# Chunk states from three rounded products, and one sum per half block read from PSUM, in a hybrid SSD and attention trunk

## The chip, the cores and the metric

The kernel runs on one core of one Trainium2 chip. The metric is the device time of one execution in microseconds, taken as the median of several runs. Engines are named as the profile does: PE is the matrix engine (PEld its weight loads), DVE the vector engine, ACT the scalar engine, POOL the GpSimd engine, SP the engine that issues most DMAs. On-chip memory is SBUF; products land in PSUM, which has banks of 128 x 512 float32.

## The reference

The model is a two-layer decoder trunk on 1040 tokens (16 learned meta tokens and 1024 of the sequence), width 1024. Layer 0 is a state-space mixer (Mamba-2 style, "SSD") and a gated feed-forward block with a width-3 causal convolution; layer 1 is stick-breaking attention and another such block. All is float32. Two parts matter here.

In the mixer there are 32 heads of 64 in four groups of eight; each group shares its B and C (128 states). Cut into chunks of tokens, a chunk computes

```
cb[l,s]       = sum_n C[l,n] B[s,n]
y_diag[l,h,p] = sum_s cb[l,s] * exp(a_cs[l,h]-a_cs[s,h]) * xdt[s,h,p]     (s <= l)
S[n,h,p]      = sum_l B[l,n] * exp(a_end[h]-a_cs[l,h]) * xdt[l,h,p]       (chunk state)
state         = state * exp(a_end) + S
y_off[l,h,p]  = sum_n C[l,n] * exp(a_cs[l,h]) * state_before[n,h,p]
```

In the feed-forward block, `h = conv3(u @ w_up)` is cut into two halves `g` and `val` of 2816 columns, and `silu(g) * val` goes through `w_down`.

## The kernel before

**Rounded products.** PE multiplies operands of type float32r in one pass. To keep float32 precision, the kernel writes an operand as high plus low part (high is a rounded copy made by ACT, low is the difference, made by DVE or POOL), and `mm3` (L206) adds three products: high x high, high x low, low x high. Most of the work of the kernel goes through `mm3`. Small products of the mixer are plain float32 products instead: `cb`, the chunk state `S` (L801) and the outputs `y` (L812, L814).

**The mixer.** After the first blocks, `mixer` (L825) walks over 4 groups of 9 chunks (116 tokens, the last 112). Between the parts of a chunk it places units of other work from a generator `work`: one unit is one projection of a block of 128 columns on a third of the tokens, 24 products through `mm3`, followed by a convolution (L336 on ACT, L339 on DVE, a silu at L616) or, for gate blocks, a silu (L648), a product (L655), a square (L660) and a sum (L664, L666). `SHARES` (L74) says how many units a chunk takes: two in groups 0 and 3 with a few exceptions at the ends, three or four in groups 1 and 2. The first unit of a block also issues the weights of the next block: a DMA, an ACT copy (L196) and four POOL pieces (L102, tile `wl`).

A chunk has these parts. `ssd_decays` (L735) is a generator in three steps: it loads two tiles `D` and `E` by DMA; then DVE makes differences (L754) and ACT the exponential (L755); then POOL multiplies `E` with C in four pieces. `ssd_front` (L761) makes `cb` and transposes B and x on PE, copies B to SBUF on ACT (`bk`, L780), masks `cb` (L782), makes `xdt` (L784) and the decay matrix (L785) on DVE, and the inputs decayed to the chunk's end (`xde`, two pieces) on POOL. `ssd_back` (L791) makes `S` on PE, adds it to the state on DVE (L807), makes `y` on PE, adds it to x (L816) and scales the state on POOL. The loop at L873 runs front of chunk c, then the units, then back of chunk c; while the units run, the decays of chunk c+1 are stepped, one step a unit, and what is left of them is run ahead of the next front.

All of this stands in a region whose order on PE, DVE, ACT and POOL is the order in which the program issues it. Every engine takes its instructions in that order, so a waiting instruction holds what stands behind it.

**The up projection.** `up` (L1203) does the product with `w_up` as a scheme of seven products on quarter matrices in place of eight. For each of 22 blocks and each half `t` of the tokens, `block` makes the products 0 to 6 in three PSUM banks x, y, z, with sums between: `p1 = copy(x)`, `y += p1`, `u2 = copy(y)`, `p5 = copy(z)`, `z += u2` (the third sum), then product 4 is added to y, and `p5 += y` by way of a copy `u3` (L1256), and product 5 to z and product 6 to y. Copies are ACT's (L1236), sums DVE's (L1239). The two halves alternate product by product, except in block 0, where half 0 runs alone, because the operands of half 1 (`forms`, L1077) are still being made: `forms` scales the rows with the norm's factors (L1093), makes differences (`minus`, L1117) and splits them into high parts (L1099, ACT) and low parts (L1100, DVE). It is a generator too, stepped once after each product of half 0. In block 0's half 0 the convolutions are put off (`late`). Outside the mixer's and the attention's regions a planner orders the instructions of each engine ahead of time, from their dependencies and its own costs; `behind` (L200) gives it an extra order between two instructions.

Of the kernel before, what the change touches and what calls it, by code (L numbers as in the profile page):

```python
# [8 lines left out]
F32 = mybir.dt.float32  # L9
# [4 lines left out]
P = 128  # L14
# [91 lines left out]
class Trunk:  # L106
# [628 lines left out]
    def ssd_decays(self, g, ct, c, pool):  # L735
# [19 lines left out]
        nc.scalar.activation(dk, dk, AF.Exp)  # L755
        yield
        if c:
# [3 lines left out]
    def ssd_front(self, g, x, bt, ct, c, dk, pool):  # L761
# [16 lines left out]
        if c < 8:  # L778
            bk = pool.tile([P, P], F32, tag="bk", name=self.nm("bk"), bufs=2)
            nc.scalar.activation(bk[:n], pcb[:n, P : 2 * P], AF.Copy)  # L780
        cbm = pool.tile([P, CB], F32, tag="cbm", name=self.nm("cbm"), bufs=2)
# [4 lines left out]
        if c < 8:  # L786
            xde = pool.tile([P, GH, 64], F32, tag="xde", name=self.nm("xde"), bufs=2)
            pieces(nc.gpsimd, xde[:n], xdt[:n], self.cols[:n, 2, cc, h0 : h0 + GH].unsqueeze(2).to_broadcast([n, GH, 64]), ALU.mult)
        return xdt, xde, bk

    def ssd_back(self, g, x, c, dk, ce, xdt, xde, bk, states, pool):  # L791
# [7 lines left out]
        if c < 8:  # L799
            ps = self.lg("S")  # L800
            nc.tensor.matmul(ps, bk[:n], xde[:n].rearrange("p h d -> p (h d)"), start=True, stop=True)  # L801
            psv = ps.rearrange("p (h d) -> p h d", h=GH)
            if c == 0:
                new = pool.tile([P, GH, 64], F32, tag="state", name=self.nm("state"), bufs=2)
                nc.scalar.activation(new, psv, AF.Copy)
            else:
                nc.vector.tensor_tensor(new, new, psv, op=ALU.add)  # L807
# [17 lines left out]
    def mixer(self, mx):  # L825
# [12 lines left out]
        with self.tc.tile_pool(name="ssd", bufs=3) as pool:  # L838
# [27 lines left out]
            with self.tc.manual_schedule(engines={E.PE, E.DVE, E.Activation, E.Pool}):  # L866
                ahead = self.ssd_decays(0, rows[0][5], 0, pool)
                dk, ce = next(ahead)
                for g in range(GROUPS):
                    *x, bt, ct = rows[g]  # L870
                    share, given = SHARES[g], 0
                    state = None, None
                    for c in range(9):  # L873
                        if g == c == 0:
                            next(work)
                            given = 1
                        for _ in ahead:
                            pass
                        begun = False
                        ops = self.ssd_front(g, x, bt, ct, c, dk, pool)  # L880
                        now = dk, ce
                        for _ in range(sum(share[: c + 1]) - given):
                            next(work)
                            if not begun:
                                begun = True
                                nxt = (g, ct, c + 1) if c < 8 else (g + 1, rows[g + 1][5], 0) if g < 3 else None
                                ahead = self.ssd_decays(*nxt, pool) if nxt else iter([(None, None)])
                                dk, ce = next(ahead)
                            else:
                                next(ahead, None)  # L890
                            given += 1
# [185 lines left out]
    def forms(self, layer, h, r, t, tiles, pool):  # L1077
# [11 lines left out]

        def product(ks, part):  # L1090
            c = slice(new.start, s.start + N) if part == 0 else slice(s.start + N, new.stop)
            for k in ks:
                nc.vector.scalar_tensor_tensor(h[k][:, c], h[k][:, c], self.par(gain, k), r[:, c], op0=ALU.mult, op1=ALU.mult)  # L1093

# [26 lines left out]
        if t:  # L1121
            product(range(KD // 2, KD), 0)
            yield
            product(K, 1)
            yield
            t1 = minus(b12, b11)
            product(range(KD // 2, KD), 1)
            yield
            t2 = minus(b22, t1)
# [73 lines left out]
    def up(self, layer, w0, forms, rest, pool):  # L1203
# [8 lines left out]
        def block(b, t, w, late=None):  # L1212
# [35 lines left out]
            p5 = copy(z)  # L1248
            add(z, z, u2)
            yield  # L1250
# [4 lines left out]
            yield  # L1255
            u3 = copy(product(4, y, False))  # L1256
            run(lambda: (add(p5, p5, u3), made.update(v1=conv(p5, 1, 1))))
# [809 lines left out]
```

## Time and profile before

| | us |
|---|---|
| median of 3 runs | 2845.09 (2844.49 to 2850.29) |
| the profiled execution | 2848.77 |
| its span in the trace | 2847.0 |
| PE busy | 2806.7 |
| DVE busy | 2071.6 |
| ACT busy | 1582.8 |
| POOL busy | 1572.9 |
| mean granted clock of PE | 0.997 |

The span is counted from the first to the last instruction of the profiled execution. The mixer's chunk loop lies between about 115 and 615 us, the up projection of layer 0 between about 830 and 1290 us, that of layer 1 between about 2150 and 2610 us. In rows of the time line, the first two numbers are the start and the duration; in groups of instructions of one line, min/median/max are in ns; in rows of stretches, the first column after the stretch is its length, then busy time of PE, PEld, DVE, ACT and POOL with the number of instructions, then the granted clock, the DMA share and GB/s.

### The profile page before, as it was taken

What the parts mean: (1) busy time and instruction counts of PE and PEld (TensorE: products, weight loads), DVE (VectorE), ACT (ScalarE), POOL (GpSimd) and SP (SyncE); (2) the same over time, 40 slices, a digit from 0 to 9 for tenths busy, and PEclk for the clock granted to TensorE, in tenths of its full rate; (3) what the DMA queues carried; (4) which work ended last, traced back from release to release, by engine and by line L of the source; (5) the groups of instructions that cost most, each with busy time, mean ns of one, the idle gap of its engine ahead of it and who ended that gap; (6) DMA issues with size and microseconds to landing.
All of it is one profiled execution on the core that took longest, in us unless ns stands there. A gap on an engine that the chain in (4) does not pass through costs nothing. (4 is left out here: it accounts for less than half of the span.)

```text
span 2847.0 us, 56457 instructions
## 1 busy us (share of the span) xinstructions
PE 2806.7 (99%) x21251; PEld 2690.8 (95%) x21251; DVE 2071.6 (73%) x3936; ACT 1582.8 (56%) x3077; POOL 1572.9 (55%) x2144
## 2 busy tenths in 40 slices
PE   8999999999999999999999999999999999999998
PEld 7989999999999999999999999999898999999888
DVE  5676666668487676767886888888759676667786
ACT  5555554543256565655335777777646555555433
POOL 2366455553519888867763111112354888886881
PEclk9999999999999999999999999999999999999999
DMA  4333333343412222235142222322532222225331
GB/s 119 88 112 97 116 84 124 117 137 101 116 68 95 78 79 79 78 129 181 44 153 75 77 67 71 85 70 55 186 132 82 83 75 82 75 83 185 111 104 67
DMA packets 141740, 281.78 MB, mean 99 GB/s; under 512 B 16307, under 2 KB 71740, under 8 KB 141468
## 3 DMA queue, kind: packets, MB, share of 16 engines
q1 hardware_dynamic: 135844, 267.01, 29.6%
q0 software_dynamic: 2048, 6.49, 0.6%
q10 hardware_dynamic: 3576, 4.67, 0.5%
q8 instruction: 168, 2.75, 0.4%
q14 instruction: 104, 0.85, 0.1%
HBM read 207.79 MB, written 55.42 MB: 92 GB/s over the span
## 5 line engine op out<-in xcount | busy, mean ns | idle before, releaser
L102 POOL TENSOR_TENSOR wl<-w,wh 128x256 fp32r<-128x256 f32 x760 | 676.3, 921 | 345.4 <-ACT wh L196 225.8
L209 PE MATMUL pj<-uh,wh 128*128 128x348 f32 (+2 forms) x1536 | 501.1, 327 | 3.4 <-DVE xbc L339 1.4
L210 PE MATMUL pj<-ul,wh 128*128 128x348 f32 (+2 forms) x1536 | 494.8, 322 | 0.8 <-DVE ul L320 0.8
L211 PE MATMUL pj<-uh,wl 128*128 128x348 f32 (+2 forms) x1536 | 491.9, 320 | 0.0
L209 PE MATMUL p<-bh,fh 128*128 128x262 f32 (+1 forms) x1408 | 401.6, 285 | 7.1 <-DVE p L1239 3.7
L211 PE MATMUL p<-bh,fl 128*128 128x262 f32 (+1 forms) x1408 | 401.4, 285 | 0.9 <-POOL fl L102 0.9
L210 PE MATMUL p<-bl,fh 128*128 128x262 f32 (+1 forms) x1408 | 399.6, 284 | 0.1
L102 POOL TENSOR_TENSOR fl<-x,fh 128x256 fp32r<-128x256 f32 x352 | 263.6, 783 | 192.9 <-ACT fh L1176 167.0
L210 PE MATMUL p<-bl,wh 128*128 128x262 f32 (+1 forms) x1040 | 295.6, 284 | 1.1 <-DVE bl L1100 1.1
L209 PEld LDWEIGHTS pj<-uh,wh 128*128 128x128 f32 x1536 | 288.7, 188 | 7.5 <-DVE qs L1607 3.1
L209 PE MATMUL p<-bh,wh 128*128 128x262 f32 (+1 forms) x1040 | 295.4, 284 | 0.4 <-ACT ft L1236 0.4
L211 PE MATMUL p<-bh,wl 128*128 128x262 f32 (+1 forms) x1040 | 294.3, 283 | 0.0
L210 PEld LDWEIGHTS pj<-ul,wh 128*128 128x128 f32 x1536 | 289.2, 188 | 2.4 <-DVE ul L320 1.4
L339 DVE SCALAR_TENSOR_TENSOR c<-p,params,c 128x260 f32<-128x260 f32 (+1 forms) x528 | 248.4, 480 | 57.4 <-ACT c L336 50.9
L211 PEld LDWEIGHTS pj<-uh,wl 128*128 128x128 f32 x1536 | 288.7, 188 | 0.1
L209 PEld LDWEIGHTS p<-bh,fh 128*128 128x128 f32 x1408 | 268.5, 191 | 8.1 <-DVE p L1239 4.1
L211 PEld LDWEIGHTS p<-bh,fl 128*128 128x128 f32 x1408 | 267.6, 190 | 1.7 <-POOL fl L102 1.3
L210 PEld LDWEIGHTS p<-bl,fh 128*128 128x128 f32 x1408 | 268.4, 191 | 0.5 <-DVE bl L1100 0.3
L1236 ACT ACTIVATE ft<-p 128x262 f32<-128x262 f32 (+1 forms) x352 | 133.6, 382 | 180.9 <-DVE p L1239 110.9
L210 PE MATMUL acc<-gl,wh 128*128 128x260 f32 (+1 forms) x672 | 214.2, 320 | 0.0
L211 PE MATMUL acc<-gh,wl 128*128 128x260 f32 (+1 forms) x672 | 213.2, 319 | 0.0
L209 PE MATMUL acc<-gh,wh 128*128 128x260 f32 (+1 forms) x672 | 210.8, 320 | 0.1
(337 smaller groups left out, 7689.2 us busy)
## 6 DMA issues: line engine op xcount, KB each, us to landing
w<-in_w_up SPq DMA_DIRECT2D x88, 512.0 KB
w<-in_w_down SPq DMA_DIRECT2D x44, 512.0 KB
w<-in_w_in SPq DMA_DIRECT2D x40, 512.0 KB
E<-ea_d SPq DMA_DIRECT2D x32, 464.0 KB
D<-acs_d SPq DMA_DIRECT2D x32, 420.5 KB
g<-c SPq DMA_DIRECT2D x88, 130.0 KB
g<-c SPq DMA_DIRECT2D x88, 128.0 KB
b<-g SPq DMA_DIRECT2D x16, 520.0 KB
```

Source lines behind the costliest of these rows:

```text
L102: done.append(eng.tensor_tensor(out[:, c], x[:, c], y[:, c], op=op))
L209: self.behind(mm(out, wh, uh, start=first, stop=False, skip_group_check=joins), tie, "behind the sums of squares")
L210: mm(out, wh, ul, start=False, stop=False, skip_group_check=joins)
L211: self.last_mm = mm(out, wl, uh, start=False, stop=last, skip_group_check=joins)
L339: ins = nc.vector.scalar_tensor_tensor(out, ps[:, o + i : o + i + n], wcol(i), out, op0=ALU.mult, op1=ALU.add)
L1236: nc.scalar.activation(s[:, :N], ps[:, :N], AF.Copy)
```

## The change

Three parts.

1. The chunk state `S`: `bk` and `xde` are split into high and low parts (`bk` with its low part made by DVE from PSUM; `xde` high on ACT and low on DVE, in a new function `split_xde` called at the end of the front), and `S` is made by `mm3` on them. The buffers are single.
2. In the chunk loop, the last step of the decays of a chunk (POOL's `E` pieces), where it has not run between units, is issued behind the front, so behind `xde`; only the step with DVE's differences and ACT's exponential must be ahead of the front.
3. In the up projection, `p5 += u3` reads bank y itself instead of a copy of it, except in half 0 of block 0; and in `forms` for half 1, the second set of four row products and the differences behind it are issued one step later, with the four products ordered behind the third sum of block 0's half 0 on DVE.

```diff
@@ ssd_decays
-        yield
+        yield "decays"
@@ ssd_front
-            bk = pool.tile([P, P], F32, tag="bk", name=self.nm("bk"), bufs=2)
-            nc.scalar.activation(bk[:n], pcb[:n, P : 2 * P], AF.Copy)
+            bk = pool.tile([P, 2, P], F32R, tag="bk", name=self.nm("bk"), bufs=1)
+            nc.scalar.activation(bk[:n, 0], pcb[:n, P : 2 * P], AF.Copy)
+            tt(bk[:n, 1], pcb[:n, P : 2 * P], bk[:n, 0].bitcast(F32), op=ALU.subtract)
...
-            xde = pool.tile([P, GH, 64], F32, tag="xde", name=self.nm("xde"), bufs=2)
-            pieces(nc.gpsimd, xde[:n], xdt[:n], self.cols[:n, 2, cc, h0 : h0 + GH].unsqueeze(2).to_broadcast([n, GH, 64]), ALU.mult)
+            xde = [pool.tile([P, GH, 64], dt, tag=t, name=self.nm(t), bufs=1) for t, dt in (("xdh", F32R), ("xdl", F32R), ("xde", F32))]
+            pieces(nc.gpsimd, xde[2][:n], xdt[:n], self.cols[:n, 2, cc, h0 : h0 + GH].unsqueeze(2).to_broadcast([n, GH, 64]), ALU.mult)
+            self.split_xde(xde, c)
         return xdt, xde, bk
+
+    def split_xde(self, xde, c):
+
+        hi, lo, t = (t[: CH[c][1]] for t in xde)
+        self.nc.scalar.activation(hi, t, AF.Copy)
+        self.nc.vector.tensor_tensor(lo, t, hi.bitcast(F32), op=ALU.subtract)
@@ ssd_back
-            nc.tensor.matmul(ps, bk[:n], xde[:n].rearrange("p h d -> p (h d)"), start=True, stop=True)
+            hi, lo = (t[:n].rearrange("p h d -> p (h d)") for t in xde[:2])
+            self.mm3(ps, bk[:n, 0], bk[:n, 1], hi, lo, True, True)
@@ mixer
+                        if not decayed:
+                            next(ahead)
+                        begun = False
+                        ops = self.ssd_front(g, x, bt, ct, c, dk, pool)
                         for _ in ahead:
                             pass
-                        begun = False
-                        ops = self.ssd_front(g, x, bt, ct, c, dk, pool)
...
+                                decayed = nxt is None
                             else:
-                                next(ahead, None)
+                                decayed |= next(ahead, None) == "decays"
@@ forms
-        def product(ks, part):
+        def product(ks, part, tie=None):
...
+                self.behind(ins, tie, "behind the third sum")
...
             product(K, 1)
             yield
+            yield
+            product(range(KD // 2, KD), 1, self.third_sum)
             t1 = minus(b12, b11)
-            product(range(KD // 2, KD), 1)
-            yield
             t2 = minus(b22, t1)
@@ up, block
-            add(z, z, u2)
+            self.third_sum = add(z, z, u2)
...
-            u3 = copy(product(4, y, False))
+            product(4, y, False)
+            u3 = y if late is None else copy(y)
             run(lambda: (add(p5, p5, u3), made.update(v1=conv(p5, 1, 1))))
```

More of the change, by code (lines that the diff above doesn't have):

```diff
@@ L868, in mixer @@
                 dk, ce = next(ahead)
+                decayed = False
                 for g in range(GROUPS):
@@ L1088, in forms @@
         b11, b12, b21, b22 = [[b[:, c] for b in rows] for rows in (b1, b2) for c in (slice(0, N), slice(FN, N2))]
-        def product(ks, part):
+        def product(ks, part, tie=None):
             c = slice(new.start, s.start + N) if part == 0 else slice(s.start + N, new.stop)
             for k in ks:
-                nc.vector.scalar_tensor_tensor(h[k][:, c], h[k][:, c], self.par(gain, k), r[:, c], op0=ALU.mult, op1=ALU.mult)
+                ins = nc.vector.scalar_tensor_tensor(h[k][:, c], h[k][:, c], self.par(gain, k), r[:, c], op0=ALU.mult, op1=ALU.mult)
+                self.behind(ins, tie, "behind the third sum")
         last = [self.after_factors, None]
```

## The prediction

> **What bounds the kernel now.** I read the page first, then busy time by stretch, then the time lines of the engines round one chunk of the state-space part.
>
> ```profile
> span 2847.0 us, 56457 instructions
> PE 2806.7 (99%) x21251; PEld 2690.8 (95%) x21251; DVE 2071.6 (73%) x3936; ACT 1582.8 (56%) x3077; POOL 1572.9 (55%) x2144
> ```
> ```profile
> 137.00:203.00 66.00, 66.00 (x513) 60.70 (x513) 49.37 (x128) 38.00 (x52) 45.20 (x64) 1.00 0.40 115
> 2188.00:2206.00 18.00, 14.82 (x113) 14.64 (x112) 14.96 (x22) 9.77 (x20) 15.11 (x22) 0.91 0.23 81
> ```
>
> TensorE is busy for 99% of the span, so only two things can shorten it: less matmul time, or one of the few places where PE stands still. In the first stretch (chunks 2 to 7 of group 0) PE never idles, but DVE is busy 49.37 of 66 us, so its slack is 25% and no more. The second stretch, in the up projection of layer 1, is the largest stall behind the start: 3.2 us idle and the granted clock at 0.91.
>
> **The change part by part: the state product.**
>
> ```profile
> L801 PE MATMUL S<-xde,bk x64: 590/592/697, 122.6 to 596.8; 116*128 116x512 f32 x64
> ```
> ```profile
> 145.17 1.02 PE L801 MATMUL S<-xde,bk 116*128 116x512 f32 x2
> ...
> 156.44 1.02 PE L801 MATMUL S<-xde,bk 116*128 116x512 f32 x2
> 157.39 0.42 PE L812 MATMUL y<-D,xdt 116*64 116x116 f32 x4
> ```
> ```profile
> 2649.68 0.40 PE L209 MATMUL acc<-gh,wh 128*128 128x512 f32 x1
> ...
> 2650.37 0.40 PE L209 MATMUL acc<-gh,wh 128*128 128x512 f32 x1
> ```
>
> The 32 float32 products are 64 records, two passes each, and hold PE for 157.39 - 156.44 = 0.95 us. Three rounded products of the same width come 0.69 us apart as a set (2649.68 to 2650.37). I add the 0.09 us by which 0.95 exceeds two passes of 0.43 (the step to the narrow y weights): 0.79 us. So PE work falls by 0.16 x 32 = 5.1 us. This counts only where PE is what the chunk waits for.
>
> **The split in front of it.** One chunk of group 0, DVE, then ACT, then POOL; the first POOL row is chunk 0, where nothing stood ahead of the inputs:
>
> ```profile
> 150.87 0.27 DVE L782 TENSOR_TENSOR cbm<-cb,past 116x116 f32<-116x116 f32 x1
> 151.06 0.68 DVE L784 TENSOR_TENSOR xdt<-px,cols 116x512 f32<-116x512 f32 x1
> 151.66 1.27 DVE L785 TENSOR_TENSOR D<-D,cbm 116x928 f32<-116x928 f32 x1
> 153.47 1.81 DVE L339 SCALAR_TENSOR_TENSOR xbc<-pj,params,xbc 128x348 f32<-128x348 f32 x3 [0.55 <-ACT xbc L336]
> 157.31 1.80 DVE L339 SCALAR_TENSOR_TENSOR xbc<-pj,params,xbc 128x344 f32<-128x344 f32 x3 [2.02 <-ACT xbc L336]
> 159.03 1.60 DVE L754 TENSOR_SCALAR D<-D,cols 116x116 f32<-116x116 f32 x8
> ...
> 162.12 0.28 DVE L782 TENSOR_TENSOR cbm<-cb,past 116x116 f32<-116x116 f32 x1
> ```
> ```profile
> 152.80 0.64 ACT L336 ACTIVATE xbc<-pj,params 128x348 f32<-128x348 f32 x1 [2.25 <-PE pj L211]
> 153.46 1.28 ACT L616 ACT_TABLE_LOAD   x1
> 154.75 0.50 ACT L616 ACTIVATE xbc<-xbc 128x348 f32<-128x348 f32 x1
> 156.64 0.64 ACT L336 ACTIVATE xbc<-pj,params 128x344 f32<-128x344 f32 x1 [1.39 <-PE pj L211]
> ...
> 161.70 1.06 ACT L196 ACTIVATE wh<-w 128x1024 fp32r<-128x1024 f32 x1
> ```
> ```profile
> 120.52 2.00 POOL L102 TENSOR_TENSOR xde<-xdt,cols 116x256 f32<-116x256 f32 x2 [14.44 <-DVE xdt L784]
> ```
> ```profile
> 151.26 3.50 POOL L102 TENSOR_TENSOR E<-E,xbc 128x232 f32<-128x232 f32 x4
> 154.72 1.18 POOL L102 TENSOR_TENSOR xde<-xdt,cols 116x256 f32<-116x256 f32 x2
> ```
>
> Today xde ends at 155.90 and S starts at 156.44, behind four E pieces of 3.50 us. The change puts xde ahead of E, but adds three links: an ACT copy of 116x512 (0.60 us, an estimate: a little over half of the 1.06 us of the 128x1024 copy), a DVE subtraction of 116x512 (0.68 us, by xdt), and the low part of bk (0.27 us, by cbm, 0.20 us of which DVE is held). All of them are issued in the front part, so behind the waiting copy on ACT stand the weight copy, the first taps (L336), the table load and the silu of the next units; behind the waiting subtraction on DVE stand the other taps (L339), the next decays (L754), the state sum and the skip. These lead to the next chunk's xdt. That is a ring through DVE, POOL and ACT in which PE takes no part.
>
> Its length for this chunk, from cbm to cbm: bk's low part 0.20, cbm to xdt 0.19, xdt to xde 0.76 (its 0.68 and a handover), xde 2.00 because D x cbm runs beside it, handover and copy 0.65. Then ACT decides: L336, table load, silu and L336 again take 0.55 + 1.28 + 0.42 + 0.64 = 2.89, and DVE's second taps start 0.05 later (DVE itself would be free 0.5 us sooner). Then DVE alone: 159.03 - 157.31 = 1.72 for the taps and 162.12 - 159.03 = 3.09 for decays, state and skip. The sum is 11.55 us. Where a weight copy (1.06 us) stands in it, 12.6; a block has three units and a chunk two, so that is two chunks in three: 12.3 on average. PE's step today is 156.44 - 145.17 = 11.27 us. So PE, which sits 1.1 us ahead of the low part's end at first (156.67 for the second product against 150.87 + 0.20 + 0.19 + 0.76 + 2.00 + 0.65 + 0.05 + 0.68 = 155.40, with some 0.2 for handovers), loses about 1.0 us a chunk in six chunks, less that 1.1: +4.9 us. Chunk 0 waited for xde already and now waits for copy and subtraction: 1.33 less 0.16 and what the second and third products overlap, +1.0. Chunk 1 +0.5. Chunk 8 has one unit and waits for DVE already; by the same delay +2.0:
>
> ```profile
> 210.44 0.42 PE L812 MATMUL y<-D,xdt 112*64 112x112 f32 x3 [1.47 <-DVE D L785]
> ```
>
> **Group 0: 4.9 + 1.0 + 0.5 + 2.0 = +8.4 us.**
>
> Group 3 has the gate units in the same place:
>
> ```profile
> 557.69 0.46 ACT L648 ACTIVATE z<-pj 128x348 f32<-128x348 f32 x1 [1.22 <-PE pj L211]
> ```
> ```profile
> 558.57 0.80 DVE L666 TENSOR_TENSOR z<-z,z 128x344 f32<-128x344 f32 x1 [1.98 <-ACT z L660]
> 559.29 0.93 DVE L655 TENSOR_TENSOR xbc<-xbc,z 128x348 f32<-128x348 f32 x1
> 562.35 0.92 DVE L666 TENSOR_TENSOR z<-z,z 128x348 f32<-128x348 f32 x1 [2.13 <-ACT z L660]
> ...
> 566.72 0.27 DVE L782 TENSOR_TENSOR cbm<-cb,past 116x116 f32<-116x116 f32 x1
> ```
>
> Ring: 3.80 to the copy's end as above, table load 1.28, z to L666 0.88, L666 and L655 0.72 + 0.93, square and handover 0.51, then 566.72 - 562.35 = 4.37: 12.5 us, more with a weight copy, against the 11.27 of a two-unit chunk. Seven chunks would lose 9 us, but the group starts with several us of slack (its first chunks come after three units); I take **+4 us** (bounds 0 and 9). Groups 1 and 2 have three or four units a chunk, 15 to 19 us, so the ring has room: there the 16 x 0.16 = 2.6 us are gained, less about 0.9 each for a PSUM bank that a late first tap may hold: **-0.8 us**. The moved E pieces (3.5 us) end about 5.5 us after xdt, still before y needs them. The single buffers of bk and the split cost nothing: their reader, S of the chunk before, precedes cb on PE. The mixer in all: 8.4 + 4 - 0.8 = +11.6 us, bounds -7 (no ring, and the few waits for xde gone) and +20.
>
> **The sum from the bank.**
>
> ```profile
> L1239 DVE TENSOR_TENSOR p<-p,ft x176: 417/435/440, 835.1 to 2595.7; 128x262 f32<-128x262 f32 x88, 128x258 f32<-128x258 f32 x88
> L1239 DVE TENSOR_TENSOR ft<-ft,ft x88: 415/827/5627, 844.6 to 2599.9; 128x262 f32<-128x262 f32 x44, 128x258 f32<-128x258 f32 x44
> ```
> ```profile
> 2191.20 5.96 DVE L1239 TENSOR_TENSOR ft<-ft,ft 128x258 f32<-128x258 f32 x2
> ```
> ```profile
> 2202.69 0.55 PE L209 MATMUL p<-bh,fh 128*128 128x258 f32 x1 [3.18 <-ACT c L1227]
> ```
>
> In 86 of 88 half blocks the ACT copy of the fourth product goes, and the sum reads PSUM: 0.83 us becomes 0.44. Nearly all of it lies under PE, so it is worth nothing, but one of these sums took 5.6 us beside POOL's work, and its late result led to the 3.2 us stall; and at a granted clock of 0.91 over 18 us another 1.6 to 1.7 us went. A sum with a PSUM operand never passed 0.44 us. So **-5.1 us** against the profiled execution. The next reader of that bank, product 6, starts three products later, 4 us, so the later release has cover.
>
> [...]
>
> **The third sum.**
>
> ```profile
> 2153.65 3.26 DVE L1093 SCALAR_TENSOR_TENSOR h<-h,params,r 128x256 f32<-128x256 f32 x8
> 2156.82 1.44 DVE L1117 TENSOR_TENSOR ft<-h 128x258 f32<-128x258 f32 x4
> 2158.17 0.43 DVE L1239 TENSOR_TENSOR p<-p,ft 128x258 f32<-128x258 f32 x1
> ```
> ```profile
> 2158.66 0.39 PE L209 MATMUL p<-bh,fh 128*128 128x258 f32 x1 [1.84 <-DVE p L1239]
> ```
> ```profile
> 2165.92 2.51 DVE L1100 TENSOR_TENSOR bl<-h,bh 128x514 fp32r<-128x514 f32 x4
> ```
>
> The sum moves ahead of four products and four differences, 1.6 + 1.4 us, and the 1.84 us wait goes. But DVE runs without a break here, the same work ends at the same time, and PE next needs these low parts, up to 2168.4. The wait moves on, it does not go: 0, bounds -4 (both layers in full) and +1.
>
> **Sum.** 2848.77 (the profiled execution, 3.7 us over the runs' median of 2845.09) + 11.6 - 5.1 + 0 = **2855.3 us**; if the median runs had no such long sum, the mixer alone gives 2856.7 from 2845.09.
>
> **Rivals.** *The ring fits under PE* (faster): the split is done before S comes. Then -5.1, some -1.9 for xde waits, -5.1, up to -4: 2832.7. For it: DVE idles 0.55 + 2.02 us in the chunk shown. Against: those waits are for PE's projections and are spent by the 1.7 us that DVE waits for the copy. *xde runs at 1.18 us instead of 2.00* (same): the ring is 0.8 shorter, 11.5 on average, which leaves about +3 in group 0, nothing in group 3 and the -0.8, the whole 2845.9. It decides if D x cbm leaves POOL alone; 120.52 speaks against it. *The low part is blocked by the E pieces* (slower yet): with 0.5 us more in each of 14 chunks, 2862.3.
>
> Chances: forecast 0.50, blocked low part 0.13, fast xde 0.22, ring hidden 0.15. So slower by over 0.2% (5.7 us, about what this kernel's measurement can tell) 0.63, within 0.22, faster 0.15. The range 2839 to 2866 reaches into the second and third rival; that of the forecast alone is 2850 to 2862.
>
> **What would show it.** Right: PE waits before S (L801's successors) on ACT's copy and DVE's low part in groups 0 and 3, with chunk steps over 12 us there and 0.16 us shorter in groups 1 and 2; no sum on L1239 over 0.5 us in up; the third sum some 3 us earlier and a new wait for bl. Wrong: no PE wait before S, or xde at 1.2 us beside D x cbm.

## The result, and the profile after

The changed kernel takes **2871.42 us** (median of five runs, 2870.69 to 2876.17) against 2844.49 us for the kernel before on the same chip: a ratio of 1.0094, 95% interval 1.0082 to 1.0105. It is slower, as forecast, but by 27 us where 10 were forecast, and outside the range given (2839 to 2866). The profiled execution of it took 2876.17 us. The head of its page, and busy time by stretch for most of chunks 2 to 7 of group 0 (columns: stretch, length, busy time and count of PE, PE's weight loads, DVE, ACT and POOL, granted PE clock, DMA share, GB/s):

```profile
span 2874.4 us, 56436 instructions
PE 2818.0 (98%) x21283; PEld 2705.3 (94%) x21283; DVE 2079.3 (72%) x4000; ACT 1568.0 (55%) x3023; POOL 1571.3 (55%) x2144
```
```profile
148.00:218.00 70.00, 66.36 (x525) 60.38 (x523) 56.58 (x136) 40.15 (x57) 46.81 (x64) 1.00 0.41 101
```

PE, never idle in these chunks before, now stands 3.6 us of 70; DVE has gone from 75% to 81%. The time lines of DVE, ACT, POOL and PE round chunk 3 of group 0:

```profile
157.42 0.26 DVE L783 TENSOR_TENSOR cbm<-cb,past 116x116 f32<-116x116 f32 x1
157.61 0.68 DVE L785 TENSOR_TENSOR xdt<-px,cols 116x512 f32<-116x512 f32 x1
158.21 1.11 DVE L786 TENSOR_TENSOR D<-D,cbm 116x928 f32<-116x928 f32 x1
161.06 1.13 DVE L797 TENSOR_TENSOR xdl<-xde,xdh 116x512 fp32r<-116x512 f32 x1 [1.74 <-ACT xdh L796]
162.11 3.61 DVE L339 SCALAR_TENSOR_TENSOR xbc<-pj,params,xbc 128x348 f32<-128x348 f32 x6
165.64 1.60 DVE L754 TENSOR_SCALAR D<-D,cols 116x116 f32<-116x116 f32 x8
...
168.93 0.27 DVE L783 TENSOR_TENSOR cbm<-cb,past 116x116 f32<-116x116 f32 x1
...
181.41 0.26 DVE L783 TENSOR_TENSOR cbm<-cb,past 116x116 f32<-116x116 f32 x1
```
```profile
160.39 0.63 ACT L796 ACTIVATE xdh<-xde 116x512 fp32r<-116x512 f32 x1 [3.49 <-POOL xde L102]
160.93 0.62 ACT L336 ACTIVATE xbc<-pj,params 128x348 f32<-128x348 f32 x1
```
```profile
158.43 1.93 POOL L102 TENSOR_TENSOR xde<-xdt,cols 116x256 f32<-116x256 f32 x2 [0.75 <-DVE xdt L785]
160.32 3.04 POOL L102 TENSOR_TENSOR E<-E,xbc 128x232 f32<-128x232 f32 x4
```
```profile
161.08 0.51 PE L209 MATMUL S<-xdh,bk 116*128 116x512 f32 x1 [0.41 <-ACT xdh L796]
162.24 0.50 PE L210 MATMUL S<-xdl,bk 116*128 116x512 f32 x1 [0.66 <-DVE xdl L797]
```

The ring is there, link by link: xdt, xde at 1.93 us beside D x cbm, the copy xdh, the low part xdl, then six taps in a row, decays, and the next cbm 11.51 us later. The copy waits for xde, xdl for the copy, and PE for both. From chunk 1 on the steps from cbm to cbm are 12.47, 12.88 and 11.51 us in turn, 12.3 on average, as forecast. Longer than in the forecast is xdl: 1.13 us beside POOL's E pieces instead of 0.68 (a rival had foreseen it).

Where the 27 us lie can be read from the start of each S product in the two traces, which is the same place of the work. The shift of S (after less before) is 8.59 us at chunk 7 of group 0, 13.31 at chunk 0 of group 1, 21.67 at chunk 0 of group 3 and 27.90 at chunk 7 of group 3; all behind it together is 0.5 us shorter. So the mixer costs 27.9 us, not 11.6: group 0 with its chunk 8 +13.3 (forecast 8.4), groups 1 and 2 +8.4 (forecast -0.8), group 3 +6.2 (forecast 4). About 0.6 us of the first term lies ahead of the chunk loop: the kernel with the mixer alone, below, has a shift smaller by that much from the first S on.

Two things hold most of the difference. First, some of the new waits of PE are followed by a lower granted clock. PE's waits for y of chunk 8 of group 0, for the squares' sum and for a held bank in group 1, and stretches behind the first and the last:

```profile
221.27 0.56 PE L821 MATMUL y<-D,xdt 112*64 112x112 f32 x2 [3.44 <-DVE D L786]
...
285.86 0.56 PE L676 MATMUL ms<-z,ones 128*128 128x348 f32 x1 [1.06 <-DVE z L666]
...
339.26 0.58 PE L209 MATMUL pj<-uh,wh 128*128 128x348 f32 x1 [2.54 <-DVE xbc L339]
```
```profile
221.27:225.00 3.73, 3.73 (x34) 3.45 (x35) 1.92 (x5) 1.20 (x1) 0.00 (x0) 0.50 0.09 36
339.26:342.70 3.44, 3.44 (x12) 3.44 (x13) 3.37 (x7) 1.66 (x2) 3.44 (x7) 0.51 0.11 18
```

After a wait of 2.54 us PE works for 3.44 us at half the clock (0.51 in the row), which by that clock is 1.7 us more, an estimate. Between 104 and 640 us the trace of before has no stretch under full clock; the changed kernel has five (from 137.9, 219.9, 339.3, 489.5 and 574.8 us). Each is 3.41 or 3.42 us long by half-microsecond stretches of the same view, the second twice that. Half of each, taken over the time in which PE worked (the second began 1.4 us before PE did), makes 1.7 + 2.7 + 1.7 + 1.7 + 1.7 = 9.5 us, an estimate.

Not all of that stays in the total. Behind the first stretch PE waits again at S of chunks 3, 5 and 6 (0.41, 0.20 and 0.57 us for the copy), so there the ring sets its time, and the ring did not get longer by the stretch: the kernel without E products, below, has no stretch there and the same steps from cbm to cbm. That leaves at most 7.8 us, and no run tells apart how much of these stayed.

Second, a chunk of three units in groups 1 and 2 has a ring too. DVE and POOL between two chunks of group 1:

```profile
316.43 0.27 DVE L783 TENSOR_TENSOR cbm<-cb,past 116x116 f32<-116x116 f32 x1
...
324.19 3.80 DVE L754 TENSOR_SCALAR D<-D,cols 116x116 f32<-116x116 f32 x8
...
333.07 0.27 DVE L783 TENSOR_TENSOR cbm<-cb,past 116x116 f32<-116x116 f32 x1
```
```profile
324.73 2.62 POOL L102 TENSOR_TENSOR E<-E,xbc 128x232 f32<-128x232 f32 x4
```

From cbm to cbm it is 333.07 - 316.43 = 16.64 us, against 14.94 for PE's step between S of chunks 4 and 5. The eight decays L754 take 3.80 us beside POOL's weight pieces and E pieces (1.60 us in the rows of group 0 above). After two such chunks the first unit's taps are late, the bank is held, and PE waits, once each in groups 1 and 2: 2.54 and 2.52 us, some 4.2 us each time with the stretch at half clock.

In the up blocks both edits do what they say, and nothing comes of it. The group of the sums from the bank, the one long DVE instruction of layer 0 and PE behind it, and PE's waits at the third sum's place:

```profile
L1253 DVE TENSOR_TENSOR ft<-ft,p x86: 408/421/429, 886.5 to 2627.0; 128x262 f32<-128x262 f32 x43, 128x258 f32<-128x258 f32 x43
```
```profile
903.09 5.56 DVE L339 SCALAR_TENSOR_TENSOR c<-ft,params,c 128x260 f32<-128x260 f32 x1
```
```profile
909.04 0.39 PE L209 MATMUL p<-bh,wh 128*128 128x262 f32 x1 [3.30 <-DVE ft L1253]
...
872.55 0.39 PE L209 MATMUL p<-bh,fh 128*128 128x262 f32 x1 [0.92 <-ACT bh L1113]
877.36 0.39 PE L209 MATMUL p<-bh,wh 128*128 128x262 f32 x1 [0.36 <-ACT ft L1250]
878.47 0.47 PE L210 MATMUL p<-bl,wh 128*128 128x262 f32 x1 [0.71 <-DVE bl L1114]
```

The sums are at 0.42 us and none over 0.43. A 5.6 us instruction is there all the same: a tap on L339, one of those that read ft from SBUF, and PE waits 3.30 us behind it. The third sum's wait in layer 0 (1.87 us in the trace of before) has become waits for bh, ft and bl.

### The profile page after: what moved, and what is told of

Same layout as the page of the kernel before. It is cut to its first block, busy times and chain, and to the rows that moved or that the text cites. A ratio compares the mean times of both kernels' runs of the same rounds, so it can differ in the third digit from the quotient of the medians.

```text
span 2874.4 us, 56436 instructions
## 1 busy us (share of the span) xinstructions
PE 2818.0 (98%) x21283; PEld 2705.3 (94%) x21283; DVE 2079.3 (72%) x4000; ACT 1568.0 (55%) x3023; POOL 1571.3 (55%) x2144
## 4 chain that ended last, share of the span: by engine, by line
PE 77%; DVE 11%; ACT 5%; POOL 4%; issue 3%; DMA 1%; DVEq 0%; ACTq 0%; POOLq 0%
PE p L209 10%; PE p L211 10%; PE p L210 10%; PE acc L209 8%; PE acc L211 8%; PE acc L210 8%; PE pj L209 5%; PE pj L210 4%; PE pj L211 4%; PE po L1727 2%; PE lg L1670 2%; DVE D L754 2%; PE wT L1704 2%; DVE kp L1681 2%; DVE xbc L339 1%
## 5 line engine op out<-in xcount | busy, mean ns | idle before, releaser
L339 DVE SCALAR_TENSOR_TENSOR c<-p,params,c 128x260 f32<-128x260 f32 (+1 forms) x528 | 248.8, 479 | 84.5 <-ACT c L336 81.1
L209 PEld LDWEIGHTS pj<-uh,wh 128*128 128x128 f32 x1536 | 290.0, 189 | 13.3 <-ACT xbc L336 7.2
L1253 DVE TENSOR_TENSOR p<-p,ft 128x262 f32<-128x262 f32 (+1 forms) x176 | 76.4, 435 | 182.2 <-ACT ft L1250 125.1
```

Of the source, the lines that this page charges most:

```text
L209: self.behind(mm(out, wh, uh, start=first, stop=False, skip_group_check=joins), tie, "behind the sums of squares")
L339: ins = nc.vector.scalar_tensor_tensor(out, ps[:, o + i : o + i + n], wcol(i), out, op0=ALU.mult, op1=ALU.add)
L1253: add = lambda o, x, y: tt(o[:, :N], x[:, :N], y[:, :N], op=ALU.add)
```

## The experiments

My theory at the start: all of the loss is in the mixer, through the order in which the split is queued on ACT and DVE; the products save 0.16 us each; the up blocks are neutral. "Shift" below is that of S against the trace of before, in us, at four places:

| kernel | median us | ratio to before (95%) | g0 c7 | g1 c0 | g2 c7 | g3 c7 |
|---|---|---|---|---|---|---|
| changed | 2871.42 | 1.0094 (1.0082, 1.0105) | 8.59 | 13.31 | 21.84 | 27.90 |
| mixer alone | 2871.90 | 1.0088 (1.0075, 1.0101) | 7.96 | 12.70 | 21.17 | 27.17 |
| up blocks alone | 2845.53 | 0.9998 (0.9990, 1.0007) | 0.67 | 0.71 | 0.71 | 0.68 |
| products without split | 2840.16 | 0.9985 (0.9974, 0.9996) | -0.89 | -0.68 | -3.17 | -4.19 |
| order on POOL alone | 2844.95 | 0.9996 (0.9987, 1.0005) | -0.66 | 1.41 | 1.42 | 0.56 |
| late split | 2847.69 | 1.0007 (0.9998, 1.0016) | 2.62 | 4.82 | 2.32 | 4.39 |
| late split, E first | 2852.51 | 1.0026 (1.0016, 1.0037) | 6.33 | 6.31 | 3.81 | 8.72 |
| late low part alone | 2888.25 | 1.0151 (1.0136, 1.0165) | 12.59 | 13.18 | 25.35 | 41.87 |
| E first | 2893.62 | 1.0173 (1.0159, 1.0187) | 21.87 | 24.01 | 33.50 | 48.53 |
| groups 1 and 2 alone | 2841.73 | 0.9992 (0.9983, 1.0001) | -0.36 | -0.36 | -2.85 | -3.04 |
| no E products | 2856.29 | 1.0044 (1.0030, 1.0058) | 7.81 | 10.75 | 8.27 | 11.76 |
| no table loads | 2868.96 | 1.0086 (1.0072, 1.0100) | 4.77 | 9.56 | 18.18 | 24.56 |
| neither | 2852.25 | 1.0028 (1.0019, 1.0038) | 2.43 | 4.28 | 1.79 | 5.67 |

Rows two to five, six to nine and ten to thirteen each shared a chip with runs of the kernel before, whose medians there were 2845.45, 2844.82 and 2844.41 us. The longer runs of before reach 2850.7 us.

### The change taken apart

Mixer alone: the up blocks of before under the changed mixer (cut, against the changed kernel).

```diff
+            t1 = minus(b12, b11)
+            product(range(KD // 2, KD), 1)
             yield
-            product(range(KD // 2, KD), 1, self.third_sum)
-            t1 = minus(b12, b11)
             t2 = minus(b22, t1)
...
-            product(4, y, False)
-            u3 = y if late is None else copy(y)
+            u3 = copy(product(4, y, False))
```

> Only the chunk states (split, three products, decayed inputs ahead of E) are changed; the up blocks are those of before. Theory (the loss is all in the mixer: the ring through DVE, POOL and ACT in groups 0 and 3, plus waits for held banks in groups 1 and 2): the starts of S shift by +13 us over group 0, +8 over groups 1 and 2, +6 over group 3, so about 27 us slower than before, 2871 to 2873. Rival (part of the loss comes from the up blocks): less than 22 us slower.

Up blocks alone: the mixer of before under the changed up blocks (cut, against the kernel before).

```diff
+            yield
+            product(range(KD // 2, KD), 1, self.third_sum)
             t1 = minus(b12, b11)
-            product(range(KD // 2, KD), 1)
-            yield
             t2 = minus(b22, t1)
...
-            u3 = copy(product(4, y, False))
+            product(4, y, False)
+            u3 = y if late is None else copy(y)
```

> Only the up blocks are changed (bank sum and third sum ahead); the mixer is that of before. Theory (both moves only shift waits, and the long blocked DVE instruction was a rare event of one execution that can hit another line): within 3 us of before, 0 to -3. Rival (my prediction's term: the sum from the bank takes 5.1 us away in every run): -5 or more. Rival (the bank sum costs, since the bank is released later): slower.

Measured: 2871.90 and 2845.53 us. The mixer alone carries the whole loss, the up blocks alone change nothing that can be measured, and the two add up. The trace of the up blocks alone shows why my 5.1 us did not come: its sums from the bank are short, and a tap is long instead.

```profile
2210.90 4.43 DVE L339 SCALAR_TENSOR_TENSOR c<-ft,params,c 128x256 f32<-128x256 f32 x1 [0.28 <-ACT c L336]
```

How much such an instruction costs is told by the length of the up stages, first product to last. Without a costly one they take 457.6 to 458.1 us in layer 0 and 453.9 to 454.3 in layer 1, whichever code they have. The profiled execution of before had 458.14 and 458.73; the changed kernel's had 462.74 and 454.25; the kernel with the mixer alone, with the old sums, 459.25 and 454.11, though one of its sums took 5.59 us. With the late low part, below, layer 0 took 464.72 us beside a tap of 7.82 us. Of the fourteen traces twelve have such an instruction: with the old sums it is always a sum (five of 3.8 to 5.6 us in three of five traces, and no tap over 2 us), with the sum from the bank always a tap (sixteen of 3.0 to 7.8 us in nine traces, and no sum). So most executions meet one, it costs up to 7 us or nothing according to where it falls, and taking the sums out of its way moved it to the taps.

### The products and the order on POOL

Products without a split: POOL writes the decayed inputs rounded, and all three products read the same pair.

```diff
-            bk = pool.tile([P, P], F32, tag="bk", name=self.nm("bk"), bufs=2)
+            bk = pool.tile([P, P], F32R, tag="bk", name=self.nm("bk"), bufs=2)
...
-            xde = pool.tile([P, GH, 64], F32, tag="xde", name=self.nm("xde"), bufs=2)
+            xde = pool.tile([P, GH, 64], F32R, tag="xde", name=self.nm("xde"), bufs=2)
...
-            nc.tensor.matmul(ps, bk[:n], xde[:n].rearrange("p h d -> p (h d)"), start=True, stop=True)
+            xr = xde[:n].rearrange("p h d -> p (h d)")
+            self.mm3(ps, bk[:n], bk[:n], xr, xr, True, True)
```

> Three products of rounded parts without a split: POOL writes the decayed inputs rounded and all three products read the same rounded pair, so the low parts of bk and of the decayed inputs are left out; order of E and the decayed inputs as before. Theory (product 0.16 us cheaper, no ring): S to y 0.79 us instead of 0.95 in all 32, 3 to 5 us faster than before, 2840 to 2842. Rival (the products themselves or their rounded operands cost more elsewhere): no gain or slower.

Order on POOL alone: in the kernel before, the E pieces are issued behind the front part.

```diff
+                        if not decayed:
+                            next(ahead)
+                        begun = False
+                        ops = self.ssd_front(g, x, bt, ct, c, dk, pool)
                         for _ in ahead:
                             pass
-                        begun = False
-                        ops = self.ssd_front(g, x, bt, ct, c, dk, pool)
...
-                                next(ahead, None)
+                                decayed |= next(ahead, None) == "decays"
```

> The kernel before with the decayed inputs made ahead of E on POOL and nothing else. Theory (xde beside D x cbm takes 2.0 us instead of 1.2 but starts 3.5 us earlier; E still has several us): the waits for xde go, 0 to -2 us. Rival (the reorder itself is part of the loss, since E comes late for y or D x cbm is held up beside xde): 3 us slower or more, with PE waiting before y for E.

Measured: 2840.16 us (1.1 to 7.4 us faster than before by the interval), and 2844.95 us. The product, in the kernel without a split:

```profile
156.20 0.40 PE L209 MATMUL S<-xde,bk 116*128 116x512 f32 x1
...
156.99 0.43 PE L813 MATMUL y<-D,xdt 116*64 116x116 f32 x4
```

S to y is 156.99 - 156.20 = 0.79 us, the value of the forecast, and in nearly all chunks the shift falls by 0.15 to 0.18 us, 4.2 us in all. Both theories of this pair held: the product gains what was worked out, and the order on POOL by itself moves the total by nothing that can be told. In its trace two effects nearly cancel: the waits for xde of chunks 0 and 1 are gone (shift -0.66), but chunk 8 waits 1.94 us instead of 1.47 and a stretch at half clock follows (0.50 from 211.0 to 214.0 us, shift +1.41 behind it).

### Where the split stands

Late split: the changed kernel, with copy and low part issued after the chunk's first projection unit.

```diff
-            self.split_xde(xde, c)
...
                             next(work)
                             if not begun:
                                 begun = True
+                                if c < 8:
+                                    self.split_xde(ops[1], c)
```

> The changed kernel with one edit: copy and low part of the decayed inputs are issued after the first projection unit of the chunk instead of ahead of it, so that they stand behind that unit's taps on ACT and DVE, not in front of them. Same instructions, same count. Theory (the loss is the order: the split holds back the taps, the next decays and the held banks): PE needs the parts some 8 us later and nothing waits for them, so the product's 0.16 us is gained in all 32 and the ring is gone, 2838 to 2843. Rival (the added work itself, 0.9 us of DVE and 0.7 us of ACT a chunk and its contention with POOL, is too much for groups 0 and 3 wherever it stands): 2850 or more.

The same with the E pieces ahead of the decayed inputs, as before the change (the diff of the order, backwards):

> As the run before it in this call, but with the E pieces ahead of the decayed inputs on POOL, as in the kernel before. Theory: the decayed inputs end at 155.9 us of the chunk of group 0 in the trace of before, the copy then ends about 0.2 us behind the place where S starts and holds the second unit's taps up a little: 2846 to 2858. Rival (with the split behind the first unit the order on POOL no longer matters): 2838 to 2843.

The low part alone late, the copy left in front:

```diff
         self.nc.scalar.activation(hi, t, AF.Copy)
+
+    def low_xde(self, xde, c):
+
+        hi, lo, t = (t[: CH[c][1]] for t in xde)
         self.nc.vector.tensor_tensor(lo, t, hi.bitcast(F32), op=ALU.subtract)
...
                             if not begun:
                                 begun = True
+                                if c < 8:
+                                    self.low_xde(ops[1], c)
```

> The changed kernel with the low part alone issued after the first unit; the copy stays ahead of it on ACT. It tells ACT's half of the wait from DVE's. Theory (in groups 0 and 3 ACT's queue decides, as the prediction had it; in groups 1 and 2 the taps stood behind the low part on DVE): groups 1 and 2 come back to -0.16 us a chunk without their two 4 us waits, groups 0 and 3 keep 8 to 14 us of their 19; 2853 to 2861. Rival (DVE's half decides everywhere): 2838 to 2845. Rival (ACT's half decides everywhere): 2866 or more.

The changed kernel with E first and the split where the change has it:

> The changed kernel with the E pieces ahead of the decayed inputs on POOL again, split at its changed place. Theory (the ring runs through POOL): it gets 3.5 us longer by the E pieces less 0.8 us because the inputs no longer run beside D x cbm, so some 2.7 us more for each of 14 chunks of groups 0 and 3, and more held banks: 2895 to 2915. Rival (the order on POOL does not lie on the way): within 5 us of the changed kernel.

Measured: 2847.69, 2852.51, 2888.25 and 2893.62 us.

The late split takes 24 of the 27 us back with the same instructions, so nearly all of the loss is the order and not the added work. But it does not reach the 2838 to 2843 that I expected, nor the rival's 2850. In groups 1 and 2 all 16 steps are 0.15 to 0.18 us shorter, no bank is held, and that though L754 takes 3.8 us there too. The rest is in groups 0 and 3. In chunk 0 of group 0 the decayed inputs themselves end late (xde at 123.6 us), so PE waits 1.29 us for the copy, as in the changed kernel, and a stretch of low clock follows from 125.6 us (0.50 from 126.0 to 129.0 us); and chunk 8 waits longer than before (1.96 us against 1.47), and another follows:

```profile
213.66 0.42 PE L820 MATMUL y<-D,xdt 112*64 112x112 f32 x3 [1.96 <-DVE D L786]
```
```profile
213.66:217.70 4.04, 4.04 (x38) 3.76 (x39) 2.72 (x8) 1.79 (x3) 0.00 (x0) 0.58 0.30 84
```

Half a microsecond more of waiting stands here with 1.7 us more behind it (shift 2.62 at chunk 7, 4.82 at chunk 0 of group 1). With E first (2852.51 us, as expected) every chunk of group 0 but chunk 2 waits again for copy or low part.

The late low part was the worst miss: 2888 where I expected 2853 to 2861; the rival by which ACT's half decides everywhere had 2866 or more. DVE and PE in one chunk of group 0:

```profile
175.66 1.81 DVE L339 SCALAR_TENSOR_TENSOR xbc<-pj,params,xbc 128x348 f32<-128x348 f32 x3 [3.22 <-ACT xbc L336]
177.38 1.28 DVE L801 TENSOR_TENSOR xdl<-xde,xdh 116x512 fp32r<-116x512 f32 x1
```
```profile
178.72 0.50 PE L210 MATMUL S<-xdl,bk 116*128 116x512 f32 x1 [1.70 <-DVE xdl L801]
```

The copy in front still holds up the first taps on ACT, DVE idles 3.22 us for them, and only then comes the low part: what it filled before, DVE's wait for ACT, is now empty, and its own 1.28 us stand just ahead of S. I had read the low part as a burden on DVE; in its changed place it was nearly free. That the copy on ACT is what cost is argued from this, not shown: no run moved the copy alone.

E first confirms the ring through POOL, but not my figure for it: in group 0 the shift grows from 1.27 to 21.87 us over seven chunks, 2.94 each, against 1.02 in the changed kernel. That is 1.92 us more a chunk, where the E pieces less the shorter xde gave 2.7, and the total came out 1.4 us below my lower bound. Why it is less is open.

### What lengthens the ring

No E products: POOL's four pieces a chunk are left out.

```diff
-        if c:
-            pieces(nc.gpsimd, ce, ce, ct[:, t0 : t0 + n].unsqueeze(1).to_broadcast([P, GH, n]), ALU.mult)
```

> The changed kernel without POOL's products E x C (the off-chunk part of y then reads the bare decays): POOL is free beside the low part of the decayed inputs. It tells whether the low part's 1.13 us (0.69 where POOL is free) is what lengthens groups 0 and 3. Theory (in the ring of a chunk, DVE and ACT decide by the same time: without the blocked 0.44 us ACT's taps still start the rest): the low part falls to 0.7 us but the chunks 2 to 7 of group 0 gain at most 0.2 us each, and the whole gains 1 to 5 us by chunk 8 and decays that are no longer held up: 2866 to 2871. Rival (the blocked low part is the excess): 14 chunks x 0.45 = 6 us or more, 2865 or less.

No table loads: a copy for the silu of the mixer's projections.

```diff
-            self.open.append(lambda: self.behind(nc.scalar.activation(t, t, AF.Silu), self.silu_tie, "behind the factors"))
+            self.open.append(lambda: self.behind(nc.scalar.activation(t, t, AF.Copy if self.mixing else AF.Silu), self.silu_tie, "behind the factors"))
...
+                self.mixing = True
```

> The changed kernel with the silu of the projections in the mixer's loop replaced by a plain copy, so that group 0 has no ACT table loads (1.28 us each, two a chunk) and ACT's half of its ring is 1.28 us shorter; the gates keep their silu. Theory (ring of group 0: DVE's half is 11.5 us, ACT's half 11.5 or 12.6 with a weight copy; only the last can gain): chunks 2 to 7 of group 0 fall from 12.1 to about 11.5 us a step, so 3 to 4 us faster than the changed kernel, and some tenths in groups 1 and 2: 2865 to 2869. Rival (ACT's half decides alone): 1.0 us or more in each chunk until PE bounds at 11.1, 2860 or less. Rival (ACT does not lie on the ring): no change.

Both:

> Both of the edits before: no products E x C and no silu in the mixer's loop. Theory (with both halves shorter, DVE's at 11.05 and ACT's under it, the ring of group 0 falls under PE's step of 11.1): group 0 adds nothing after its first two chunks, the gain is larger than the two single ones together in chunks 2 to 7; 2858 to 2863 in all. Rival (the halves do not tie): the gains of the two runs simply add.

Measured: 2856.29, 2868.96 and 2852.25 us. Groups of DVE's decays and low parts, first of the changed kernel, then without E (busy us, mean ns of one, idle before):

```profile
L754 DVE TENSOR_SCALAR D<-D,cols 116x116 f32<-116x116 f32 x256 | 73.4, 358 | 0.0
L797 DVE TENSOR_TENSOR xdl<-xde,xdh 116x512 fp32r<-116x512 f32 x32 | 27.9, 873 | 60.3 <-ACT xdh L796 60.3
```
```profile
L754 DVE TENSOR_SCALAR D<-D,cols 116x116 f32<-116x116 f32 x256 | 56.5, 293 | 0.0
L795 DVE TENSOR_TENSOR xdl<-xde,xdh 116x512 fp32r<-116x512 f32 x32 | 22.2, 692 | 57.4 <-ACT xdh L794 57.4
```

Without E the low part is back at 0.69 us, and 15 us go, where I expected 1 to 5. That is the rival's number, but not its place. The ring of group 0 is as long as with E; cbm of the same chunks as above:

```profile
157.06 0.27 DVE L781 TENSOR_TENSOR cbm<-cb,past 116x116 f32<-116x116 f32 x1
...
168.57 0.27 DVE L781 TENSOR_TENSOR cbm<-cb,past 116x116 f32<-116x116 f32 x1
...
181.05 0.27 DVE L781 TENSOR_TENSOR cbm<-cb,past 116x116 f32<-116x116 f32 x1
```

The steps are 11.51 and 12.48 us, the same as in the changed kernel: the blocked low part was not what held these chunks, as the theory had it. Most of the gain is in groups 1 and 2, where the decays of the slow chunks take 1.6 to 1.8 us instead of 3.4 to 3.8, the step from cbm to cbm shown above falls from 16.6 to 14.9 us, which is PE's own, and both held banks and their half clock are gone (shift from group 1 chunk 0 to group 2 chunk 7: +8.5 becomes -2.5).

Without table loads the total falls by 3.3 us in the trace, as expected, and groups 1 and 2 keep their held banks. The steps of the ring, over chunks 1 to 4 of group 0, tell DVE's half of it from ACT's:

| kernel | step 1 to 2 | step 2 to 3 | step 3 to 4 |
|---|---|---|---|
| changed | 12.47 | 12.88 | 11.51 |
| no E products | 12.48 | 12.89 | 11.51 |
| no table loads | 11.85 | 11.84 | 11.42 |
| neither | 11.86 | 11.46 | 10.97 |

In the step without a weight copy on ACT (the last) either edit alone gives at most 0.09 us and both give 0.54: there DVE's half and ACT's half tie, and either alone can only give what the other allows. In the two steps with a weight copy ACT's half is the longer one. In the total both edits together came out below my 2858 to 2863; that estimate held no gain in groups 1 and 2, and the run has one (shift from 4.28 to 1.79).

### A version that should keep the gain

Three products in groups 1 and 2 alone, late split, order on POOL and up blocks as before the change.

```diff
...
+            if g in (1, 2):
+                hi, lo = (t[:n].rearrange("p h d -> p (h d)") for t in xde[:2])
+                self.mm3(ps, bk[:n, 0], bk[:n, 1], hi, lo, True, True)
...
+                                if c < 8 and g in (1, 2):
+                                    self.split_xde(ops[1], c)
```

> The kernel before with one change: three products of rounded parts in groups 1 and 2 alone, the split issued after the first unit, E ahead of the decayed inputs as before, up blocks as before; groups 0 and 3 keep the float32 product. Theory (a chunk of three or four units hides the whole split, in the late split's trace each of these 16 steps was 0.15 to 0.18 us shorter): 16 x 0.16 = 2.6 us faster than before, about 2842, and no wait before S. Rival (the single buffers or the added work cost what the products give): 2844 to 2846.

Measured: 2841.73 us, ratio 0.9992 (0.9983 to 1.0001). No wait stands at S:

```profile
340.19 0.40 PE L209 MATMUL S<-xdh,bk 116*128 116x512 f32 x1
...
340.98 0.43 PE L829 MATMUL y<-D,xdt 116*64 116x116 f32 x4
```

The trace gives 2.5 us over the 16 chunks, the median 2.7, as the theory had it; but the interval just reaches no change. The only kernel here whose interval lies wholly on the faster side is the one that leaves the low parts out. The margin is at the edge of what can be told.

## Why the prediction was right and wrong

**The product: right.** 0.79 us forecast, 0.79 measured wherever no wait stands, with the split and without.

**The ring in group 0: right in mechanism and length, wrong in PE's lead.** Forecast 11.55 us for a chunk without a weight copy, measured 11.51; forecast 12.3 on average, measured 12.3. The prediction had ACT deciding with DVE 0.5 us behind; the blocked xdl (1.13 instead of 0.68 us) used up nearly all of that half microsecond without making the ring longer. But chunks 2 to 7 were to add 4.9 us, since PE was to start 1.1 us ahead of the low part. It had no such lead: PE waits 0.70 and 0.67 us already at S of chunk 1. The shift grows by 6.7 over them, and by 6.3 without E, where no stretch of low clock stands.

**A failed step, the largest: groups 1 and 2.** "So the ring has room" was said of chunks of 15 to 19 us without working the ring out for three units. It is 16.6 us there, because the decays then fall beside POOL's pieces at 3.80 us. The price taken for a held bank, 0.9 us, was 2.5 and up to 1.7 of low clock, twice; and PE waited 1.06 us for the squares' sum at 285.86 us in group 1. Forecast -0.8, measured +8.4: 9.2 of the 16.3 us by which the mixer was underestimated. The runs without E and with the late split both give -2.5.

**A failed step: each wait was priced at its own length.** The prediction read in the trace of before that the up stall of 3.2 us was followed by a lower clock that cost another 1.7, and counted that when it took the stall away. It did not count it for the waits that it put in. Five times a stretch at half clock followed, of which up to 7.8 us stayed (3.4 of them in groups 1 and 2, counted above too). Chunk 8 shows it best: forecast 2.0; its wait grew by 3.44 - 1.47 = 1.97, and the rest of its 4.7 us is low clock. Group 3 came out at 6.2 where 4 was forecast, with one such stretch, inside the bounds of 0 and 9.

The length of a wait alone does not tell whether a half clock follows. In the trace of before a wait of 1.87 us was followed by it, while that of 1.84 us in layer 1 and that of 1.47 us in chunk 8, both shown in the prediction, were not:

```profile
842.71 0.39 PE L209 MATMUL p<-bh,fh 128*128 128x262 f32 x1 [1.87 <-DVE p L1239]
```
```profile
840.22:843.63 3.41, 1.54 (x13) 1.34 (x12) 3.41 (x11) 1.00 (x3) 0.00 (x0) 1.00 0.00 0
843.63:847.04 3.41, 3.41 (x18) 3.41 (x17) 3.41 (x12) 3.12 (x9) 0.00 (x0) 0.50 0.02 5
2154.35:2157.76 3.41, 2.46 (x21) 2.25 (x19) 3.41 (x10) 0.85 (x3) 0.00 (x0) 1.00 0.00 0
2157.76:2161.17 3.41, 2.52 (x20) 2.52 (x21) 3.41 (x11) 2.21 (x7) 0.00 (x0) 1.00 0.00 0
208.75:212.16 3.41, 1.94 (x34) 1.66 (x32) 3.28 (x6) 3.10 (x4) 0.00 (x0) 1.00 0.26 96
```

Each row is 3.41 us long, as is the stretch at half clock (0.50) in the second. In the first, which holds the wait of 1.87 us, PE works 1.54 us. The wait of 1.84 us lies partly in each of the next two: PE works 2.46 and 2.52 us, and the clock stays at 1.00. In the row of chunk 8, with 1.94 us of work, it stays too (1.00 also in the 3.41 us behind). That the work within such a span decides is a reading of these rows and not shown: no run changed that alone. In the trace of the changed kernel the stretches between 104 and 640 us begin at 137.94, 219.86, 339.32, 489.51 and 574.84 us, which is 24, 35, 44 and 25 times 3.413 us apart; why is open.

Idle times of 1.87, 1.96 and 2.54 us, each in a row above, were followed by a stretch at half clock. Nor was it always one long wait: in chunk 1 of the changed kernel two short ones (0.70 and 0.67 us) stand 0.5 us apart ahead of one.

PE at S of chunk 1 of the changed kernel, and the stretch behind it:

```profile
135.72 0.50 PE L209 MATMUL S<-xdh,bk 116*128 116x512 f32 x1 [0.70 <-ACT xdh L796]
136.89 0.50 PE L210 MATMUL S<-xdl,bk 116*128 116x512 f32 x1 [0.67 <-DVE xdl L797]
```
```profile
137.94:141.35 3.41, 3.41 (x34) 3.12 (x31) 2.78 (x6) 3.19 (x5) 2.82 (x5) 0.50 0.00 0
```

**The blocked low part: a rival that came true beside the forecast.** It was priced at +0.5 us in each of 14 chunks, a price that no run shows. The block was there, 0.45 us long (1.13 instead of 0.68), but without E the steps of the ring in group 0 stay the same, so that price was wrong in group 0.

**The sum from the bank: -5.1 us that did not come.** The sums never pass 0.43 us, as forecast, but the long instruction is a tap in the changed kernel. The step that failed is to take one event of one execution as belonging to its line. It moved the forecast little against the median, since the profiled execution that the sum started from held that event and was itself 3.7 us over the median of its runs.

**The third sum: right.** The wait moved on, as forecast, to bh and bl among others; in the kernel with the up blocks alone the whole edit is worth nothing that can be told.

## What to carry to other kernels

When a change adds a wait on PE, price it in two parts: the wait, and the stretch of lower clock that may follow it. In one trace here it followed a wait of 1.87 us and not one of 1.84 us; so count it as a chance, with 1.7 us a stretch (an estimate, half of 3.41 us), and not as a length from which it is sure. Where PE waited again soon behind (0.41, 0.20 and 0.57 us at chunks 3, 5 and 6 of group 0), the ring's steps were the same with the stretch and without. A helper operation costs by where it is queued more than by its duration: the changed kernel costs 27 us with copy and subtraction ahead of the units and 3 with both behind the first of them, and moving the subtraction alone cost 17 more. Work out the ring of dependences through the side engines for each kind of chunk, with the durations that hold when the other engines run beside it, and do not book as a gain the removal of a single outlier that other lines can meet as well.

## What the hardware showed unexpectedly

- Not only the sums of two SBUF tensors took 5 us (5.63 in the trace of before), but also a tap that reads ft and its own sum from SBUF: 5.56 us on one where the next takes 0.48, while POOL ran pieces of 0.7 us back to back, so that it outlasts several of them.
- DVE's decays, 116x116 with per-row scalars, start 0.19 us apart when POOL is idle and 0.58 to 0.65 us apart beside its pieces (eight in 1.60 and in 3.80 us, in the rows above; the last of the 3.80 us are 0.19 us apart again, behind the E pieces).
- The half clock, as told above: after idle times under 2 us (1.87 and 1.96), once after two of 0.70 and 0.67 us, and after a wait of 1.87 us but not after one of 1.84 us in the same trace.
